# Weight splits in the attention stage, tied behind the last issued exponential

## The chip, the cores and the metric

The kernel runs on one NeuronCore of a Trainium2 chip. Its metric is the device time of one execution in microseconds (us), from launch to end. TensorE (PE) multiplies; PEld is the loading of its stationary operand, which overlaps it; VectorE (DVE), ScalarE (ACT) and GpSimd (POOL) work beside it; SyncE (SP) and POOL issue the DMAs. Each engine takes its instructions in one fixed order that is set when the program is built, and semaphores hold an instruction back until its operands are there.

## The reference, cut to what matters

The kernel computes two transformer-like blocks over 1024 tokens of width 1024, in float32. The stage that the change touches is the differential attention of the second block: eight heads, each with two score maps of head dimension 64, and values of width 128.

```python
q = rope_partial(rms_norm(q, q_norm), cos, sin) * (ATTN_HEAD_DIM ** -0.5)
k = rope_partial(rms_norm(k, k_norm), cos, sin)
for blk in range(s // Q_BLOCK):
    q0, q1 = blk * Q_BLOCK, (blk + 1) * Q_BLOCK
    sc = jnp.einsum('bqhmd,bkhmd->bhmqk', q[:, q0:q1], k[:, :q1])
    p = jax.nn.softmax(jnp.where(mask, sc, NEG_INF), axis=-1)
    w = p[:, :, 0] - lam * p[:, :, 1]
    outs.append(jnp.einsum('bhqk,bkhd->bqhd', w, v[:, :q1]))
o = rms_norm(jnp.concatenate(outs, axis=1), subln) * (1.0 - lambda_init)
mixed = sigmoid(g_lru) * y_lru + sigmoid(g_attn) * y_attn
```

q, k and v, and the two gates g_lru and g_attn, are products of the normalised input with slices of w_in.

## The kernel before, in words

A float32 product is made of three matmuls on split operands: a value is kept as a rounded high part and a low part, and high x high, high x low and low x high are added (`mm3`, lines 171 to 175). A weight is split where it is loaded: `stream` and `load_split` take one of two raw buffers, SP issues a DMA of 512 KB, ACT copies the rounded high part (tile wh) and DVE subtracts it from the raw data for the low part (tile wl). There are four buffers of wh and four of wl. The copy of wh therefore waits for the DMA and for the last matmul on the tile that had its buffer; the next DMA into the same raw buffer waits for DVE's subtraction.

Attention runs in four passes p of two heads each. A pass has 16 units: query tiles of 128 rows in the order 0, 7, 1, 6, 2, 5, 3, 4, taken in pairs, and for each pair both heads hh. A unit goes through these steps:

- `unit_qk` (line 1481): scores into PSUM (tile sc, two buffers), row maxima on DVE (tile st), and two exponentials on ACT (tile e, line 1528), one for each map.
- `unit_mix`: DVE combines the two maps in place in e.
- `unit_tr`: PE transposes the mixed weights (tile pt), ACT and DVE split them (wth, wtl).
- `unit_pv`: PE multiplies with V into tile po; `unit_o` adds the result on DVE.

Between the steps of units, `fill` takes work from a generator of fillers, which keeps PE busy while ACT and DVE work on a unit. The fillers are the key and value projections (`k_tiles`, tile pj, 24 matmuls of 128x256 for 128 rows), the query projections (`q_tile`, also pj) and the gate projections (`gate_unit`, tile pg, 24 matmuls of 128x512). The weights of k and v for a pass are asked for at the head of `k_tiles` through `w2` (four wh and wl tiles, two of k and two of v), those of q after the fourth value tile, and those of a gate through `gate_w`. `need` runs the rest of a pass's projections alone when the next pass begins.

The Python code states dependencies and priorities; a scheduler that works when the program is built puts the instructions of each engine in order. `issue_after(ins)` adds an edge: every instruction traced inside the block that runs on the engine of `ins` must stand behind `ins` in that engine's order. It adds no semaphore.

Of the kernel before, what the change touches and what calls it, by code (L numbers as in the profile page):

```python
# [16 lines left out]
AF = mybir.ActivationFunctionType  # L17
# [112 lines left out]
class Model:  # L130
# [906 lines left out]
    def lru(self):  # L1037
        nc, A = self.nc, self.A
        D = self.dram
        self.ghb = [D.tile([128, 1024], F32, name=f"gh{i}") for i in range(8)]  # L1040
        self.tab = [D.tile([128, 1024], F32, name=f"ta{i}") for i in range(16)]
        self.x0 = None
        self.w4p = self.pool("w4")
        W = self.w4 = self.w4p.__enter__()
        self.at0p = self.pool("at0")
# [153 lines left out]
    def attention(self):  # L1199
        nc, A = self.nc, self.A  # L1200
        self.ob = [self.dram.tile([128, 1024], F32, name=f"ob{i}") for i in range(8)]
        self.t0b = [self.dram.tile([128, 1024], F32, name=f"t0{i}") for i in range(8)]
        W = self.w4
        with self.pool("at1") as T1, self.pool("at") as T, \
# [8 lines left out]

            alone = [False, 0]

            def w2(src):
                return [self.stream(W, src[j], [128, 4, 256]) for j in range(2)]

            def proj(w, i, out):

# [49 lines left out]
            gst = {}  # L1270

            def gate_w(j):
                if j < 16 and j not in gst:
                    g, n = gates[j]
                    gst[j] = self.stream(W, A["w_gl2" if g == 0 else "w_ga2"][n], [128, 8, 128])

            def gate_unit(u):
                j, h = divmod(u, 2)
                g, n = gates[j]
                w = gst[j]  # L1280
                if u == 1:
                    ps = PS.tile([128, 512], F32, name="pg", tag="sc")
                else:
                    ps = PJ.tile([128, 512], F32, name="pg", tag="pj")
                for k in range(8):
                    self.mm3(ps, (w[0][:, k], w[1][:, k]), self.xnc(k, h), k == 0, k == 7)
                    if k == 3 and h == 0 and j % 4:
                        gate_w(j + 1)
                    yield 0.65
                t = T.tile([128, 512], F32, name="tg", tag="tg", bufs=1)  # L1290
                self.act(t, ps, AF.Tanh, scale=0.5)
                nc.gpsimd.dma_start(out=self.tab[8 * g + n][:, h * 512:h * 512 + 512], in_=t)
# [4 lines left out]

            def k_tiles(p):
                wk = w2(A["w_k2"][p])
                wv = w2(A["w_v2"][p])  # L1300
                yield "k", p
                kh = T.tile([128, 4, 1024], F32R, name="kh", tag="kh")
# [12 lines left out]
                for n in range(8 + 2):  # L1315
                    if n < 8:
                        o = []
                        yield from proj(wk, n, o)
                        d, _ = norm_rope(o[0], n, True)
                        pend.append((n, d))  # L1320
                    if n == 1:
                        yield "v", p
                    if n > 1:
                        j = n - 2
                        o = []
                        yield from proj(wv, j, o)
                        ps = o[0].rearrange("p (h a) b -> p h (a b)", h=2)
                        self.split(V[:, j, :, 0], V[:, j, :, 1], ps)
                        finish()
                        yield 0.3  # L1330
                        if j == 3:
                            WQ[p] = w2(A["w_q2"][p])
# [19 lines left out]
            def fillers():  # L1352

                gate_w(0)
                yield from gate_unit(0)
                yield from gate_unit(1)
                for p in range(4):
                    yield from k_tiles(p)
                    gate_w(4 * p + 1)
                    for n, i in enumerate(tiles):  # L1360
                        q = q_tile(p, i)
                        for c in q:
                            if c == -1:
                                break
                            yield c
                        if n > 1:
                            yield from gate_unit(8 * p + n)
                        else:
                            yield 0.1
                        yield from q  # L1370
                        yield "q", p, n

                    if p < 3:
                        yield from gate_unit(8 * p + 8)
                        yield from gate_unit(8 * p + 9)
# [105 lines left out]
    def unit_qk(self, unit, QS, KV):  # L1481
        nc = self.nc
        T, PS, PT, _, ma, mb, lamn, _ = self.at
        p, i, hh = unit
        self.mark(f"at{p}.{i}.{hh}")
        qs, rq = QS[p, i]
        kh, kl, _ = KV[p]
        W = (i + 1) * 128
        wc = max(W, 256)
        one = wc <= 512  # L1490
        pieces = [(0, wc)] if one else [(0, wc // 2), (512, wc // 2)]
        st = T.tile([128, 8], F32, name="st", tag="st", bufs=3)
        rqh = rq[:, 2 * hh:2 * hh + 2]
        es, vs = [], []
        sc = None
        for m in range(2):
            a = 2 * hh + m
            if m == 0 or not one:
                sc = PS.tile([128, 2, 512], F32, name="sc", tag="sc")
            base = sc[:, m] if one else sc.rearrange("p a b -> p (a b)")  # L1500
            k0 = 0
            for pi, (o, n) in enumerate(pieces):
                last = pi == len(pieces) - 1
                nc.tensor.matmul(base[:, o:o + n], qs[:, a], kh[:, a, k0:k0 + n], start=True, stop=False)
                nc.tensor.matmul(base[:, o:o + n], qs[:, a], kl[:, a, k0:k0 + n], start=False, stop=not last)
                if last:

                    end = 128 if i == 0 else o + n
                    nc.tensor.matmul(base[:, end - 64:end], ma, mb, start=False, stop=True)
                k0 += n  # L1510
            if not one:
                v = sc[:, :, 0:W // 2]
                nc.vector.tensor_reduce(out=st[:, m:m + 1], in_=v, op=OP.max, axis=AX.XY)
                self.stt(st[:, m:m + 1], st[:, m:m + 1], -1.0, rqh[:, m:m + 1], OP.mult, OP.mult)
            vs.append(sc[:, m, 0:W] if one else v)
        if one:
            nc.vector.tensor_reduce(out=st[:, 0:2], in_=sc[:, :, 0:W], op=OP.max, axis=AX.X)
            self.stt(st[:, 0:2], st[:, 0:2], -1.0, rqh, OP.mult, OP.mult)
        for m in range(2):
            e = T.tile([128, 512 if one else 1024], F32, name="e", tag=f"e{m}{int(one)}", bufs=1)  # L1520
            ev = e[:, 0:W] if one else e[:, 0:W].rearrange("p (a b) -> p a b", a=2)
            self.act(ev, vs[m], AF.Exp, bias=st[:, m:m + 1], scale=rqh[:, m:m + 1], accum=st[:, 2 + m:3 + m])
            es.append(e[:, 0:W])
        return {"st": st, "es": es, "i": i, "hh": hh, "po": None}

# [1028 lines left out]
```

## Time and profile before

| | |
|---|---|
| median of 3 runs | 2487.82 us (2479.79 to 2490.89) |
| profiled execution, its own time | 2485.62 us |
| span of that execution | 2483.9 us |
| PE busy | 2355.6 us, 95% |
| DVE busy | 1748.2 us, 70% |
| ACT busy | 1314.5 us, 53% |

The span is from the first to the last instruction. The attention stage takes the stretch from about 697 to 1440 us. The four passes have their first exponentials near 759, 939, 1118 and 1297 us. A busy PE is not PE at its peak, because matmuls overlap; its waits, with what ended them, are the more telling view. [...]

### The profile page before, as it was taken

How to read it: one execution, taken by the hardware profiler on the slowest of the kernel's cores; microseconds unless marked ns; L12 is line 12 of the kernel's file. 1: busy time of each engine (PE TensorE's matmuls, PEld its weight loads, DVE VectorE, ACT ScalarE, POOL GpSimd, SP SyncE). 2: the span in 40 equal slices, each digit the busy share in tenths (PEclk: the TensorE clock that was granted, in tenths of full speed). 3: DMA queues.
4: the chain of work that ended last, by engine and by line, in shares of the span. 5: the costliest groups of instructions: out<-in, count | busy, mean ns of one | idle time of the engine just before them, and what ended most of it. 6: DMA issues, size and time to landing. Idle time of an engine off the chain costs nothing. (4 is left out here: it accounts for less than half of the span.)

```text
span 2483.9 us, 35045 instructions
## 1 busy us (share of the span) xinstructions
PE 2355.6 (95%) x13016; PEld 1936.7 (78%) x13016; DVE 1748.2 (70%) x3344; ACT 1314.5 (53%) x2102; POOL 341.5 (14%) x363
## 2 busy tenths in 40 slices
PE   8999989999999999999899899999997999999998
PEld 6888868787888898798798678887885777666765
DVE  9667767677875666666666744235667999898987
ACT  5344532445645455454445432134435888787886
POOL 1011114100021021121121100000011111111111
PEclk9999999999999999999999999999998999999999
DMA  6322353322221111110111456532267999999992
GB/s 222 99 68 67 117 179 127 123 78 84 72 77 39 64 45 42 51 52 35 56 51 40 144 199 221 176 119 77 85 244 271 368 376 373 371 372 359 368 371 66
DMA packets 103838, 394.32 MB, mean 159 GB/s; under 512 B 14129, under 2 KB 33073, under 8 KB 79089
## 3 DMA queue, kind: packets, MB, share of 16 engines
q1 hardware_dynamic: 85008, 335.18, 37.5%
q0 software_dynamic: 18656, 56.88, 7.3%
q8 instruction: 104, 1.70, 0.3%
q14 instruction: 70, 0.57, 0.1%
HBM read 339.07 MB, written 61.31 MB: 161 GB/s over the span
## 5 line engine op out<-in xcount | busy, mean ns | idle before, releaser
L166 DVE TENSOR_TENSOR wl<-raw,wh 128x1024 fp32r<-128x1024 f32 (+1 forms) x496 | 587.7, 1209 | 130.3 <-ACT wh L154 126.1
L154 ACT ACTIVATE wh<-raw 128x1024 fp32r<-128x1024 f32 (+1 forms) x496 | 512.1, 1048 | 250.0 <-PE pj L174 67.2
L173 PE MATMUL pj<-wh,xnh 128*128 128x256 f32 x768 | 222.2, 289 | 2.1 <-ACT tg L154 1.0
L175 PE MATMUL pj<-wh,xnl 128*128 128x256 f32 x768 | 217.2, 283 | 0.0
L174 PE MATMUL pj<-wl,xnh 128*128 128x256 f32 x768 | 217.0, 283 | 0.0
L175 PE MATMUL pg<-wh,xl 128*96 128x512 f32 x512 | 201.3, 393 | 1.6 <-DVE xl L166 1.6
L174 PE MATMUL pg<-wl,xh 128*96 128x512 f32 x512 | 202.6, 396 | 0.0
L173 PE MATMUL pg<-wh,xh 128*96 128x512 f32 x512 | 200.2, 400 | 0.9 <-ACT xh L154 0.9
L173 PEld LDWEIGHTS pj<-wh,xnh 128*128 128x128 f32 x768 | 145.4, 189 | 3.8 <-ACT pc L154 2.5
L174 PEld LDWEIGHTS pj<-wl,xnh 128*128 128x128 f32 x768 | 145.2, 189 | 0.0
L175 PEld LDWEIGHTS pj<-wh,xnl 128*128 128x128 f32 x768 | 145.1, 189 | 0.0
L154 ACT ACTIVATE e<-sc,st,ss 128x1024 f32<-128x1024 f32 (+7 forms) x128 | 105.7, 829 | 54.2 <-DVE st L158 42.4
L178 POOL TENSOR_TENSOR ss<-ss,mhalf 128x4 f32<-128x4 f32 (+1 forms) x68 | 72.7, 1069 | 343.5 <-DVE ss L163 318.4
L173 PE MATMUL pd<-wh,ah 128*96 128x512 f32 x248 | 98.2, 400 | 16.6 <-ACT y L154 16.6
L175 PEld LDWEIGHTS pg<-wh,xl 128*96 128x96 f32 x512 | 83.1, 162 | 38.6 <-DVE xl L166 3.2
L173 PEld LDWEIGHTS pg<-wh,xh 128*96 128x96 f32 x512 | 83.0, 162 | 33.8 <-ACT xh L154 1.3
L174 PEld LDWEIGHTS pg<-wl,xh 128*96 128x96 f32 x512 | 82.8, 162 | 32.4
L173 PE MATMUL pg<-xnh,wh 128*128 128x512 f32 x256 | 104.9, 410 | 0.4 <-ACT kv L154 0.2
L175 PE MATMUL pg<-xnh,wl 128*128 128x512 f32 x256 | 102.6, 401 | 0.0
L173 PE MATMUL pj<-xnh,wh 128*128 128x512 f32 x256 | 102.2, 400 | 0.0
L174 PE MATMUL pg<-xnl,wh 128*128 128x512 f32 x256 | 102.2, 399 | 0.0
L174 PE MATMUL pj<-xnl,wh 128*128 128x512 f32 x256 | 101.2, 396 | 0.0
(998 smaller groups left out, 6327.5 us busy)
## 6 DMA issues: line engine op xcount, KB each, us to landing
raw<-in_w_gu SPq DMA_DIRECT2D x128, 1024.0 KB, 15.3
raw<-in_w_dn SPq DMA_DIRECT2D x64, 1024.0 KB, 15.9
raw<-in_w_out SPq DMA_DIRECT2D x16, 512.0 KB, 4.6
ta<-tg POOLq DMA_DIRECT2D x32, 256.0 KB, 2.5
t<-ta SPq DMA_DIRECT2D x14, 512.0 KB, 3.9
raw<-in_w_ga SPq DMA_DIRECT2D x12, 512.0 KB, 3.7
raw<-in_w_v SPq DMA_DIRECT2D x12, 512.0 KB, 3.5
xraw<-in_xT SPq DMA_DIRECT2D x8, 512.0 KB, 5.8
```

Of the source, the lines that this page charges most:

```text
L154: return self.nc.scalar.activation(out=out, in_=in_, func=func, **kw)
L166: return (eng or self.nc.vector).tensor_tensor(out=out, in0=a, in1=b, op=op)
L173: mm(ps, l[0], r[0], start=start, stop=False)
L174: mm(ps, l[0], r[1], start=False, stop=False)
L175: return mm(ps, l[1], r[0], start=False, stop=stop)
L178: self.nc.gpsimd.tensor_tensor(out=out, in0=in_, in1=self.mhalf[:, :w], op=OP.pow)
```

## The change

`unit_qk` now keeps the exponential that it issued last in `self.last_exp`. `w2` and `gate_w` open an `issue_after` block on it around their `stream` calls, if there is one. The last exponential runs on ACT, so the edge binds the ACT half of a split, the copy of wh; DVE's subtraction follows because it reads wh. The DMAs are on SP and are not bound.

```diff
-        self.x0 = None
+        self.x0 = self.last_exp = None
...
+            def after_exp():
+
+                return self.tc.issue_after(self.last_exp.ins) if self.last_exp else nullcontext()
+
             def w2(src):
-                return [self.stream(W, src[j], [128, 4, 256]) for j in range(2)]
+                with after_exp():
+                    return [self.stream(W, src[j], [128, 4, 256]) for j in range(2)]
...
-                    gst[j] = self.stream(W, A["w_gl2" if g == 0 else "w_ga2"][n], [128, 8, 128])
+                    with after_exp():
+                        gst[j] = self.stream(W, A["w_gl2" if g == 0 else "w_ga2"][n], [128, 8, 128])
...
-            self.act(ev, vs[m], AF.Exp, bias=st[:, m:m + 1], scale=rqh[:, m:m + 1], accum=st[:, 2 + m:3 + m])
+            self.last_exp = self.act(ev, vs[m], AF.Exp, bias=st[:, m:m + 1], scale=rqh[:, m:m + 1], accum=st[:, 2 + m:3 + m])
```

What this does to the orders is shown at two places, both at the end of the first pass. The first is ACT. In the kernel before, the copies wh_8653 and wh_8659 (key weights of the second pass) and wh_8665 (value weights) stand among the exponentials of the middle of the pass; e_8049 and e_8051 belong to query tile 2, e_8133 and e_8135 to tile 5.

```order
L154 ACTIVATE wh_8653<-raw_8655 128x1024
L154 ACTIVATE e_8049,st_8039<-sc_8040,st_8039,ss_7840 128x384
L154 ACTIVATE e_8051,st_8039<-sc_8040,st_8039,ss_7840 128x384
L154 ACTIVATE qs_8113<-pt_8108,gcol_5343 128x512
L154 ACTIVATE pc_8340<-pj_8315 128x256
L154 ACTIVATE wh_8659<-raw_8661 128x1024
L154 ACTIVATE nq_8343<-pc_8340 128x256
L154 ACTIVATE nr_8342<-pc_8340 128x512
L154 ACTIVATE wth_8141<-pt_8137 128x384
L154 ACTIVATE wh_8665<-raw_8667 128x1024
L154 ACTIVATE e_8133,st_8116<-sc_8117,st_8116,ss_8010 128x768
L154 ACTIVATE tg_8439<-pg_8354 128x512
```

In the changed kernel the same copies stand behind e_8624, the last exponential of the pass (query tile 4, second head), with the copy of the first key projection, pc_8783, behind all four.

```order
L154 ACTIVATE e_8622,st_8605<-sc_8606,st_8605,ss_8345 128x640
L154 ACTIVATE ot_8579<-pt_8574,sub_5339 128x512
L154 ACTIVATE e_8624,st_8605<-sc_8614,st_8605,ss_8345 128x640
L154 ACTIVATE wh_8653<-raw_8655 128x1024
L154 ACTIVATE wh_8659<-raw_8661 128x1024
L154 ACTIVATE wth_8631<-pt_8626 128x512
L154 ACTIVATE osq_8595<-o4_7549 128x512
L154 ACTIVATE wh_8665<-raw_8667 128x1024
L154 ACTIVATE wh_8671<-raw_8673 128x1024
L154 ACTIVATE pc_8783<-pj_8727 128x256
```

The copies moved past 16 exponentials (wh_8653) to 8 (wh_8671) on ACT; their subtractions on DVE moved with them. The second place is PE, a little ahead of that point, where it transposes the mixed weights of the unit of tile 3, first head (pt_8471 from e_8386). In the kernel before, the 24 matmuls of a key projection (pj_8836) stand in front of it, of which the first four are shown; po is a product with V, and pt_8442 turns a query tile.

```order
L1266 MATMUL pt_8442<-ident_60,nr_8342 128x128 x4
L1551 MATMUL po_8418<-V_6710,wtl_8403 128x256
L1550 MATMUL po_8418<-V_6710,wth_8402 128x256
L1551 MATMUL po_8418<-V_6710,wtl_8403 128x256
L173 MATMUL pj_8836<-wh_8653,xnh_3988 128x256
L174 MATMUL pj_8836<-wl_8654,xnh_3988 128x256
L175 MATMUL pj_8836<-wh_8653,xnl_3989 128x256
L173 MATMUL pj_8836<-wh_8653,xnh_3988 128x256
```

In the changed kernel the transposes and the next unit's scores follow the product with V directly (lines are six higher from `unit_qk` on).

```order
L1271 MATMUL pt_8442<-ident_60,nr_8342 128x128 x4
L1557 MATMUL po_8418<-V_6710,wtl_8403 128x256
L1556 MATMUL po_8418<-V_6710,wth_8402 128x256
L1557 MATMUL po_8418<-V_6710,wtl_8403 128x256
L1544 MATMUL pt_8471<-ident_60,e_8386 128x128 x4
L1510 MATMUL sc_8451<-kh_6708,qs_8447 128x320
L1511 MATMUL sc_8451<-kl_6709,qs_8447 128x320
```

Both key projections that stood between the units of the last two query tiles (pj_8727 and pj_8836, 48 matmuls) have left this stretch, and 16 matmuls of a third (pj_8797) have left the stretch after it; all now stand behind the transposes pt_8626 of the last unit but one. The ends of the second and third pass have the same moves (there 24 matmuls in place of the 16). The fourth pass has no next pass to project for.

## Rows read from the trace of the kernel before

**Rows 1.** The page's busy shares, and the clock granted in 40 slices.

```profile
PE 2355.6 (95%) x13016; PEld 1936.7 (78%) x13016; DVE 1748.2 (70%) x3344; ACT 1314.5 (53%) x2102; POOL 341.5 (14%) x363
...
PEclk9999999999999999999999999999998999999999
```

**Rows 2.** Waits of PE in the first three passes: total us, times, longest.

```profile
PE sc L1504 <- ACT e L154: 8.8, 6, 1.9
PE po L1551 <- DVE wtl L166: 6.3, 6, 1.6
PE pt L1538 <- DVE e L158: 1.8, 3, 1.4
PE po L1550 <- ACT wth L154: 1.7, 3, 0.6
```

**Rows 3.** Projections (tile pj) on PE before each pass's last units: length, busy, count.

```profile
857.80:865.50 7.70, 6.08 (x48) 1.00 0.32 104
1035.80:1043.50 7.70, 6.10 (x48) 1.00 0.32 105
1216.50:1224.10 7.60, 6.01 (x48) 1.00 0.30 103
```

**Rows 4.** The first pass's end, stretches: length; PE, PEld, DVE, ACT, POOL busy; PEclk.

```profile
857.80:865.50 7.70, 7.70 (x68) 7.70 (x67) 5.27 (x14) 3.28 (x8) 0.45 (x1) 1.00 0.32 104
865.50:873.90 8.40, 5.27 (x35) 3.92 (x33) 6.26 (x16) 2.96 (x6) 0.58 (x1) 1.00 0.00 0
873.90:881.70 7.80, 6.76 (x40) 6.12 (x41) 6.49 (x22) 4.44 (x10) 1.30 (x2) 0.78 0.00 0
881.70:891.00 9.30, 9.30 (x81) 9.30 (x80) 7.98 (x26) 5.24 (x13) 3.91 (x5) 1.00 0.15 59
```

**Rows 5.** Timeline of DVE there: start, us, operation.

```profile
862.29 0.75 DVE L158 SCALAR_TENSOR_TENSOR e<-e,st 128x512 f32<-128x512 f32 x1
863.49 0.76 DVE L158 SCALAR_TENSOR_TENSOR qs<-pt,gcol,qs 64x512 fp32r<-64x512 f32 x1
```

**Rows 6.** Timeline of PE there: transposes of the mixed weights, and one wait.

```profile
865.47 0.60 PE L1538 MATMUL pt<-ident,e 128*128 128x128 f32 x4
...
873.95 0.77 PE L1538 MATMUL pt<-ident,e 128*128 128x128 f32 x5 [1.41 <-DVE e L158]
...
881.73 0.60 PE L1538 MATMUL pt<-ident,e 128*128 128x128 f32 x4
```

**Rows 7.** Timeline of ACT: exponentials and square of the units of tiles 4 and 3.

```profile
869.45 0.89 ACT L154 ACTIVATE e<-sc,st,ss 128x640 f32<-128x640 f32 x1 [2.74 <-PE po L1551]
...
871.19 0.62 ACT L154 ACTIVATE osq<-o 128x512 f32<-128x512 f32 x1
...
881.15 0.89 ACT L154 ACTIVATE e<-sc,st,ss 128x640 f32<-128x640 f32 x1 [1.09 <-DVE oss L166]
```

**Rows 8.** Weight splits of the first three passes: count, busy us, mean ns, idle before.

```profile
L154 ACT ACTIVATE wh<-raw 128x1024 fp32r<-128x1024 f32 x26 | 27.6, 1060 | 28.5 <-PE pg L174 23.3 <-PE pj L175 5.2
L166 DVE TENSOR_TENSOR wl<-raw,wh 128x1024 fp32r<-128x1024 f32 x26 | 31.8, 1225 | 11.5 <-ACT wh L154 11.0
```

**Rows 9.** DMA issues of these passes: count, KB, median us to landing.

```profile
raw<-in_w_v SPq DMA_DIRECT2D x6, 512.0 KB, 3.5
```

**Rows 10.** Timeline of ACT at a split in mid-pass.

```profile
835.05 1.06 ACT L154 ACTIVATE wh<-raw 128x1024 fp32r<-128x1024 f32 x1 [5.91 <-PE pg L174]
836.01 0.97 ACT L154 ACTIVATE e<-sc,st,ss 128x768 f32<-128x768 f32 x1
836.98 0.58 ACT L154 ACTIVATE tg<-pg 128x512 f32<-128x512 f32 x1
837.46 0.99 ACT L154 ACTIVATE e<-sc,st,ss 128x768 f32<-128x768 f32 x1
```

**Rows 11.** Timeline of PE at the same place.

```profile
834.85 0.40 PE L175 MATMUL pg<-xnh,wl 128*128 128x512 f32 x1
837.13 0.44 PE L1504 MATMUL sc<-kh,qs 128*128 128x384 f32 x1 [1.88 <-ACT e L154]
```

## The prediction

> **What bounds the kernel now.** I read the page's busy shares first: PE is busy for 95% of the span and its clock is at the upper level in nearly every slice [rows 1]. So a time can only be gained by taking away PE's idle time or its half clock, and lost by adding to either. Next I read PE's waits in the three passes whose ends the change touches: 8.8, 6.3, 1.8 and 1.7 us, 18.6 us together [rows 2]. That is all the idle time that a better order could take away there. Then I asked what keeps PE busy at a pass's end, where both fillers and units run out. The projections do it: 48 matmuls, 6.08, 6.10 and 6.01 us, stand in the 7.7 us before the last units of each pass [rows 3], and there PE has no idle time at all (7.70 of 7.70). In the next 8.40 us, which hold no projections, PE is busy for only 5.27 [rows 4]. This second row shows what the units alone look like: PE waits for ACT and DVE.
>
> **What the change does.** Nothing is added to or removed from the arithmetic; 26 ACT copies of 1.06 us and 26 DVE subtractions of 1.23 us were there in these passes [rows 8] and are there after. They move. The block ties a split to the exponential that the code issued last. For the weights of keys and values that is the pass's very last exponential, because the code of the last unit's scores is run before the generator reaches the next `k_tiles`. So four copies per pass end, and the two key projections that need them, go from the middle of the pass to behind its end. I work out the first pass's end in four pieces; the orders of the other two ends move alike.
>
> Piece A, up to the transposes at 865.47 [rows 6]. Of the 7.7 us, 6.1 leave and 1.6 of PE work stay [rows 3, 4]. The transposes cannot follow at once: DVE finishes the mixture that they read at 862.29 + 0.75 = 863.04 [rows 5]. They can come 2.4 us earlier, so the piece is 5.3 long with 1.6 of work: 3.7 us idle, before none. The bounds are 0 (all 6.1 us come back because the softmax chain too moves forward) and 6.1 (nothing is shortened); the two rows give the value between.
>
> Piece B, to the next transposes at 873.95 [rows 6]. No filler stood here, and none does now. But the query's low part on DVE, 0.76 us, was done before the transposes of piece A, at 864.25 [rows 5], and now comes between the mixture and the next scores: 0.8. And in the new ACT order the square of 0.62 us, which stood behind two exponentials [rows 7], stands between them: 0.6. Together 1.4; bounds 0 (DVE, without the first key tile's normalisation, catches up) and 2.
>
> Piece C, to the transposes at 881.73 [rows 6]. Here 16 projection matmuls leave and the transposes move forward by as much as these took, since they only stood behind them in PE's order: 0. The upper bound is 1.9, 16 matmuls at 0.12 (6.08 over 48, about 0.125 each) with nothing gained.
>
> Piece D, behind the last exponential, which begins at 881.15 and takes 0.89 [rows 7]. In the kernel before PE had no idle time in the 9.30 us from there [rows 4]. Now the first projection waits for a copy of 1.06 and its low part for another 1.23 on DVE [rows 8]; DVE must first do the unit's own mixture, some 0.9 for 640 columns (estimate from 0.75 for 512 [rows 5]). And wth, which the product with V needs, stands behind two copies, 2 x 1.06 + 0.6 = 2.7 (the 0.6 an estimate from the square of the same width [rows 7]). So PE gets its stream back some 2.9 us after that exponential; it has transposes and a few matmuls till about then, but it reaches them half a microsecond before the exponential ends, now that nothing else delays it. I take 3.0; bounds 1.5 (only the copy's time and a wait) and 4.6 (two copies and two subtractions in a row).
>
> What hides the rest: the raw buffer of the value weights is freed by the first subtraction, at 2.9; then 3.5 us of DMA [rows 9], 1.06 and 1.23 make 8.7. Till then PE has the 48 postponed matmuls and eight products with V, 6.1 + 1.0 from 2.9 on, so till 10.0. It is covered with 1.3 us to spare, and counts nothing; beyond that, each us that the DMA is later costs one.
>
> The sum for one end: 3.7 + 1.4 + 0 + 3.0 = 8.1; for three ends 24.3.
>
> In mid-pass there is one place of 1.88 us idle [rows 11] per pass. ACT stood idle for 5.91 us behind a copy that waited for a buffer, and took 1.06 for it, while an exponential was ready that PE's scores waited for [rows 10]. The change puts that copy away: about 1.0 back. But the split of the pass's last gate weight now stands right behind the second exponential here, and PE, which runs out of gate matmuls, waits for 1.06 + 1.23 of it with only some scores and transposes to do: about 1.0 lost. I take 0, bounds -1.9 and +1.3.
>
> [...]
>
> [...] I assume as much half clock at each end as before, no more. [...]
>
> The last part of attention and the expert stage get slightly other orders too, since the scheduler starts from other times; I see no term in them that has a sign, and count 0, give or take 3.
>
> **The time.** The profiled execution took 2485.62 us, 1.7 over its span and 2.2 below the median of the runs shown, well inside their spread of 11. The sum is made against it: 2485.6 + 24.3 = 2509.9, so 2510.
>
> **The rivals.**
> - The early copies were the hindrance. For it: ACT's idle time of 28.5 us in front of copies [rows 8], and PE's 8.8 us behind exponentials [rows 2]. If those 8.8 go and the postponed projections are as good later, the time is 2476.8; if all 18.6 us of waits go, 2467.0. It decides from the point where the units' chain on ACT and DVE runs ahead of PE without help. Against it: [rows 4] shows that it does not run ahead, in just these stretches. This is the case on the other side; chance 0.10, of which 0.07 is beyond half a per cent.
> - The chain closes up. Without the key tile's normalisation DVE has less to do, so pieces A and B shrink: A 1.5, B 0, D 2.0, three times 3.5, gives 2496.1. For it: DVE is busy for 6.26 of 8.40 us and ACT for 2.96 [rows 4], so neither is full. Against: the steps follow each other, and a chain is not shortened by engines that are free between its steps. Chance 0.21.
> - The gap breeds more. Piece C pays its 1.9 and each end a further 1.7 of half clock: 8.1 + 3.6 = 11.7, three times, gives 2520.7. For it: the 0.78 behind a lesser gap [rows 4]. Against: the 1.88 us of mid-pass and its kind did not always bring a half clock; the means of the slices stay at 9 tenths or more [rows 1]. Chance 0.15.
> - That the change does not do what it says is excluded by the order: the four copies do stand behind the last exponential.
>
> **How the numbers follow.** The forecast has 0.54, with 2501 to 2517 as its own range (A from 2.5 to 4.5, B from 0.5 to 2, D from 2 to 4). A measurement here can tell about half a per cent, 12.4 us, from no change. Slower by more: the forecast and the third rival, 0.69. Within: the second rival and the small end of the first, 0.24. Faster by more: 0.07. The range for 8 in 10 goes from 2488, which takes in most of the second rival, to 2524, which takes in the third.
>
> **What would show it.** Right: at each of the three pass ends the four wh copies stand in ACT's timeline behind the pass's last exponential; between the units of the last two query tiles PE shows new waits, of 2 us and more before the transposes (for e on DVE) and before the scores (for e on ACT); then a wait of about 3 us at the first projection, for wh and wl; PE's waits in the three passes grow from 18.6 to about 40. The DMA of the value weights lands before PE asks for it. Wrong: if PE's waits there stay under 25, piece A has closed up; if the time is above 2524, look at the granted clock at the ends and at waits for the value weights; if it is below 2486, look whether the 1.88 us places have gone and the ends have not grown.

## The result and the profile after

The changed kernel takes 2517.3 us (median of 4 runs, 2515.24 to 2519.68) against 2488.2 us (4 runs, 2479.79 to 2490.89): ratio 1.0123, 95% interval [1.0097, 1.0149]. The forecast was 2510 in a range of 2488 to 2524. The profiled execution took 2517.62 us with a span of 2515.6, so there are 31.7 us of span to explain where the prediction had 24.3.

The page after, against [rows 1]: busy shares and granted clock.

```profile
PE 2367.7 (94%) x13016; PEld 1939.4 (77%) x13016; DVE 1748.3 (69%) x3344; ACT 1313.5 (52%) x2102; POOL 341.8 (14%) x363
...
PEclk9999999999999999999999999999998999999999
```

The instruction counts are those of before, and yet PE is busy for 12.1 us more: here busy time is no count of work, so a loss need not show as idle time alone.

Waits of PE in the three passes after (total, times, longest), against [rows 2]:

```profile
PE pt L1544 <- DVE e L158: 11.0, 6, 2.5
PE sc L1510 <- ACT e L154: 9.1, 12, 1.4
PE po L1556 <- ACT wth L154: 3.6, 6, 0.9
PE pt L1582 <- DVE wtl L166: 2.9, 2, 1.8
PE pj L173 <- ACT wh L154: 1.2, 1, 1.2
```

All groups of this view add to 31.4 us, before 18.6. The largest is the wait that the prediction named for piece A and B, transposes for the mixed weights of DVE. At the first pass's end PE's timeline has, against [rows 6]:

```profile
863.34 0.63 PE L1544 MATMUL pt<-ident,e 128*128 128x128 f32 x4 [1.33 <-DVE e L158]
868.03 0.50 PE L1510 MATMUL sc<-kh,qs 128*128 128x512 f32 x1 [1.35 <-ACT e L154]
872.91 1.33 PE L1544 MATMUL pt<-ident,e 128*128 128x128 f32 x5 [2.11 <-DVE e L158]
877.58 0.60 PE L1544 MATMUL pt<-ident,e 128*128 128x128 f32 x4
879.42 0.51 PE L173 MATMUL pj<-wh,xnh 128*128 128x256 f32 x2 [1.24 <-ACT wh L154]
880.85 0.38 PE L1556 MATMUL po<-V,wth 128*128 128x256 f32 x1 [0.93 <-ACT wth L154]
```

The first is the gap that the fillers had filled (piece A). The next two are in piece B, where no filler stood before either; there the kernel before had waits of its own, 1.41 us for the transposes [rows 6] and, before the scores:

```profile
870.48 0.50 PE L1504 MATMUL sc<-kh,qs 128*128 128x512 f32 x1 [1.07 <-ACT e L154]
```

They became 2.11 and 1.35. The last two lines of the changed kernel are the restart behind the last exponential. The other side of that restart is on ACT, against [rows 7]: exponential, two copies in a row (x2), and only then the copy of the attention weights that PE asks for.

```profile
877.45 0.88 ACT L154 ACTIVATE e<-sc,st,ss 128x640 f32<-128x640 f32 x1
...
878.32 1.99 ACT L154 ACTIVATE wh<-raw 128x1024 fp32r<-128x1024 f32 x2
880.22 0.58 ACT L154 ACTIVATE wth<-pt 128x512 fp32r<-128x512 f32 x1
...
884.74 1.06 ACT L154 ACTIVATE wh<-raw 128x1024 fp32r<-128x1024 f32 x1 [3.42 <-DMA raw<-in_w_v]
```

The copy of the value weights does wait for its DMA, 3.42 us, but no line of PE names it: from 880.85 to 892 PE's timeline marks no wait. That cover held.

The same 34 us of both kernels in three stretches (length; PE, PEld, DVE, ACT, POOL busy; granted clock; DMA), before and then after:

```profile
858.00:866.00 8.00, 8.00 (x70) 8.00 (x70) 5.07 (x14) 3.28 (x8) 0.95 (x1) 1.00 0.31 100
866.00:878.00 12.00, 7.83 (x45) 6.05 (x44) 9.63 (x29) 6.21 (x14) 1.09 (x2) 0.91 0.00 0
878.00:892.00 14.00, 14.00 (x115) 13.80 (x115) 11.10 (x35) 7.23 (x16) 5.14 (x6) 0.96 0.10 39
```

```profile
858.00:866.00 8.00, 6.11 (x42) 4.86 (x41) 5.99 (x13) 4.27 (x9) 0.54 (x1) 1.00 0.08 33
866.00:878.00 12.00, 8.51 (x45) 6.85 (x43) 8.93 (x27) 6.86 (x15) 1.92 (x2) 0.72 0.00 0
878.00:892.00 14.00, 11.84 (x96) 11.27 (x95) 11.10 (x24) 8.46 (x16) 2.48 (x4) 1.00 0.51 168
```

PE's idle time (length less busy) goes from 4.2 to 7.5 us, and the half clock ((1 - PEclk) x length) from 1.6 to 3.4: 5.1 us more together in these stretches; the whole end costs 5.7. Half clock stands for a granted clock of 0.50, as PEclk has it in the kernel before from 876 to 879 us: there the products with V of 128x256 start 0.21 us apart, where from 880 to 883, at 1.00, the projections of 128x256 start 0.12 apart.

Where all 31.7 us arise is read by setting the same exponential's start in both traces side by side. The shift of after against before grows by 0.8 up to the first end; by 5.7, 8.4 and 8.5 over the three ends (from the first exponential behind the mid-pass copy, 836.01 in [rows 10] and 836.75 in the changed kernel, and its counterparts, to the first one of the next pass: 938.96 became 945.38, 1118.18 became 1133.33, 1296.64 became 1320.64); by 0.3 and 0.4 between them; by 2.6 from there to the expert stage; by 5.5 in it (to the last y, 0.4 of it given back by the end of the span). The ends are 22.6 of it.

### The profile page after: what moved, and what is told of

It is laid out like the page before. It is cut to its first block, busy times and chain, and to the rows that moved or that the text cites. A ratio compares the mean times of both kernels' runs of the same rounds, so it can differ in the third digit from the quotient of the medians.

```text
span 2515.6 us, 35051 instructions
## 1 busy us (share of the span) xinstructions
PE 2367.7 (94%) x13016; PEld 1939.4 (77%) x13016; DVE 1748.3 (69%) x3344; ACT 1313.5 (52%) x2102; POOL 341.8 (14%) x363
## 5 line engine op out<-in xcount | busy, mean ns | idle before, releaser
L154 ACT ACTIVATE pc<-pj 128x256 f32<-128x256 f32 x96 | 36.5, 382 | 127.9 <-PE pj L175 123.5
```

The source lines that it names most:

```text
L154: return self.nc.scalar.activation(out=out, in_=in_, func=func, **kw)
```

## The experiments

In all of them a split keeps its arithmetic; only the exponential to which it is tied changes, so the order. "Ends" is the growth of the shift over the three ends, as above, in the profiled execution; "expert" the growth in the expert stage. "Idle" and "half clock" are PE's over the three ends in the same execution, from the exponential at 839.55 before (the next unit's first, behind the mid-pass place) and its counterparts to the first one of the next pass; the half clock is rough, about half a us an end, since PEclk has two digits. The kernel before, run beside them, had medians of 2487.82, 2487.51 and 2486.87. In the edits `exps[-1]` is the exponential issued last, so `exps[-9]` is the ninth from the end, with eight behind it; the expectations call it "nine before the last", and the names "nine back" and the like below stand for `exps[-9]` and its kind.

| keys and values tied to | gates, q | median us | ratio, 95% | ends | expert | idle | half clock |
|---|---|---|---|---|---|---|---|
| (the kernel before) | | | | 0 | 0 | 13.1 | 6.9 |
| last (the change) | last | 2517.3 | 1.0123 [1.0097, 1.0149] | 22.6 | 5.5 | 26.7 | 11.7 |
| free | last | 2502.4 | 1.0068 [1.0051, 1.0085] | 4.6 | 3.9 | 16.8 | 6.0 |
| last | free | 2515.5 | 1.0112 [1.0095, 1.0129] | 22.7 | 9.1 | 27.4 | 15.0 |
| last, one pass of three | free | 2492.6 | 1.0024 [1.0014, 1.0033] | 6.3 | -0.9 | 17.8 | 8.3 |
| values alone, last | free | 2493.9 | 1.0026 [1.0016, 1.0035] | 7.0 | 5.5 | 15.8 | 13.2 |
| third from the end (three back) | free | 2503.3 | 1.0068 [1.0054, 1.0082] | 10.9 | 9.7 | 20.6 | 9.3 |
| fifth (five back) | free | 2482.1 | 0.9978 [0.9968, 0.9989] | -0.6 | -0.6 | 16.8 | 0 |
| seventh (seven back) | free | 2483.9 | 0.9988 [0.9979, 0.9997] | -4.8 | 5.3 | 11.4 | 0 |
| ninth (nine back) | free | 2478.9 | 0.9965 [0.9951, 0.9979] | -2.6 | -1.1 | 12.0 | 5.9 |
| thirteenth (thirteen back) | free | 2490.0 | 1.0006 [0.9995, 1.0017] | 5.4 | 5.5 | 18.2 | 8.0 |
| values alone, thirteenth | free | 2485.8 | 0.9993 [0.9984, 1.0003] | -3.5 | 5.6 | 10.9 | 6.9 |
| ninth | last | 2494.8 | 1.0032 [1.0021, 1.0042] | -0.3 | 9.0 | 10.6 | 6.9 |

How far an "ends" figure can be read is shown by the kernel with one pass tied. Its first end is not touched: PE and ACT have the order of the kernel before there, and PE's waits agree within 0.02 us. Yet its shift fell by 2.5. First the kernel before, then that one:

```profile
839.55:938.96 99.41, 95.20 (x717) 89.57 (x716) 65.24 (x173) 49.70 (x104) 18.18 (x21) 0.97 0.14 49
840.67:937.55 96.88, 92.57 (x714) 87.15 (x713) 65.06 (x173) 49.50 (x104) 18.28 (x21) 1.00 0.14 49
```

The idle time is 4.2 and 4.3 us; the difference is the granted clock, 0.97 and 1.00. So one end of one execution can move by 2.5 us with no change of order, and the idle time is the steadier measure of an order.

**Which ties cost.** The first edit frees keys and values, the second frees gates and q instead:

```diff
-            def w2(src):
-                with after_exp():
+            def w2(src, tied=True):
+                with after_exp() if tied else nullcontext():
...
-                wk = w2(A["w_k2"][p])
-                wv = w2(A["w_v2"][p])
+                wk = w2(A["w_k2"][p], False)
+                wv = w2(A["w_v2"][p], False)
```

> Undoes one part: the splits of key and value weights are free again, those of query and gate weights stay tied. Theory (the loss is at the three pass ends, because the key projections that filled PE there were moved behind the last exponential): the three ends cost nothing, PE's waits before the transposes of the last units vanish, and only the other terms of the measured loss can stay, about 5 us in the expert stage and 3 in the fourth pass: 2488 to 2497 us. Rival (the gate splits, which now stand behind exponentials in mid-pass, hold the gate projections up): 2505 us or more.

> Does one part alone: the splits of key and value weights are tied, those of query and gate weights are not. Theory: nearly the whole loss, 23 us at the three ends and what the expert stage adds: 2509 to 2519 us, with the same waits at the ends as in the changed kernel. Rival (gate splits): 2486 to 2494 us.

With keys and values free 4.6 us of the ends' 22.6 stay; with only these tied all 22.7 are there, and PE's idle time is 16.8 and 27.4 us. So the ends' loss belongs to the keys and values. That the two sums agree so well is in part luck: the second kernel loses 8.9, 6.5 and 7.3 where the changed one loses 5.7, 8.4 and 8.5, with more half clock. Nor are its waits those of the changed kernel, as was expected: its order puts the next tile's scores ahead of the transposes at each end (at the first, scores at 861.18 and transposes at 863.75; in the changed kernel transposes at 863.34 and scores at 864.03), and its largest waits are those of the products with V for wth and wtl (5.6 and 4.6 us). But 2502.4 fits neither expectation: the gate ties have a price of their own, about 14 us by the medians. Of 11.8 us of span in the profiled execution 4.6 are at the ends and 3.9 in the expert stage.

**One end alone, and the values alone.** In both, gates and q are free as well. `p == 2` in place of `False` ties the keys and values of one pass. In the other kernel only `wv` is tied: the 48 key matmuls keep their place ahead of the last scores, and two copies stand behind the last exponential.

> Only the key and value splits of the third pass are tied, so one of three ends is changed. Theory: a third of the ends' loss, 8 us at the second end and none at the others, and up to 5 more if the expert stage takes the changed order: 2495 to 2503 us. Rival (the loss comes from a change of the scheduler's whole plan, not from each end): the first and third end move too, or the time is that of the changed kernel, 2510 us or more.

> Only the value weights' splits are tied, so the key projections keep their place between the last units while two of four copies and subtractions still come behind the last exponential, their DMAs being early. Theory (lost are the fillers, not the place of the copies): the ends cost 0 to 1 us each, 2488 to 2496 us with the expert stage's 5. Rival (late copies and subtractions themselves are the price, as in piece D of the prediction): 3 us or more at each end, 2500 us or more.

The tied end costs 8.1 us, the other two -2.5 and 0.8, and PE's idle time grows at the tied end alone (9.4 us, where the other two have 4.3 and 4.2): the ends are separate, and the prediction's multiplication by three holds. The time is below its range because of that -2.5, which is the clock's, and of 1.3 us gained in mid-pass. Values alone cost 1.7, 3.1 and 2.2 at the ends, between the 0 to 1 of the theory and the 3 of the rival, though the time is in the theory's range. Only 2.7 us of it is idle time of PE; the half clock grew by 6.3, where the untouched end above had 3.0 in one execution (0.97 over 99.41 us) and none in the other (1.00), so by an estimate up to 9 over three ends. So the price of late copies where the fillers stay is about 0.9 us of idle time an end, and up to 2.3 with a clock that this one execution doesn't settle.

**How late is too late.** Now keys and values are tied to an earlier exponential, with gates and q free:

```diff
-                return self.tc.issue_after(self.last_exp.ins) if self.last_exp else nullcontext()
+                return self.tc.issue_after(self.exps[-9].ins) if self.exps else nullcontext()
```

> Key and value weights stay tied, but to the exponential issued nine before the last instead of to the last; gate and query weights are free. So the four copies stand some 15 us before the pass's last units, no longer spread over mid-pass, and the 48 key projections are again between the last units but two. Theory (an end costs about 8 us because these matmuls have left the last units' gaps and because their copies come too late behind the last exponential): ends cost 0 to 2 us each, the mid-pass place of 1.88 us gains about 1.3 per pass as in the runs with only key and value weights tied, the expert stage -1 to +5: 2483 to 2493. Rival (it is the tie itself, four copies in a row ahead of a unit's work on ACT and DVE, wherever it stands): 5 us or more per end, 2500 to 2512.

> The same, tied to the exponential issued five before the last. The key projections now stand one unit later than before, between the last two units (pieces C and D filled, A and B empty). Theory (pieces A and B cost what they cost in the changed kernel, 3 to 4 us per end together, piece D with its late copies costs nothing, less 1.3 in mid-pass; expert stage -1 to +5): 2490 to 2503, between the nine-back and the last-exponential versions. Rival (the loss is all at the restart behind the last exponential, pieces A and B close up): 2483 to 2490, as with nine back. Rival (any delay costs the whole): above 2508.

> Key and value weights tied to the exponential thirteen before the last, gate and query weights free: the key projections now stand one unit earlier than before, and the stretch in front of the last units (piece A) has none of the second block. Theory (fillers are worth most where the units alone leave PE idle, which is in the last four units; earlier there are gate matmuls to fill): ends cost 0 to 3 us each, mid-pass -1.3: 2484 to 2495. Rival (earlier is never worse): at or below the nine-back version and at most 2486.

Nine back came out 4 us below its range and faster than both kernels: its ends gained 2.6 us where they were to cost 0 to 2 each. Five back missed: the key matmuls have left pieces A and B there too, as in the changed kernel, and yet the shift over its ends doesn't grow. Its 34 us at the first end:

```profile
858.00:866.00 8.00, 4.54 (x30) 3.62 (x30) 6.13 (x15) 3.83 (x10) 0.00 (x0) 1.00 0.00 0
866.00:878.00 12.00, 10.95 (x82) 10.03 (x83) 10.48 (x22) 8.66 (x16) 0.30 (x1) 1.00 0.39 125
878.00:892.00 14.00, 13.53 (x112) 13.14 (x112) 10.64 (x37) 6.56 (x16) 6.32 (x7) 1.00 0.19 64
```

Piece A is as idle as predicted, 3.5 us, but all 48 matmuls now run from 866 to 878, where the kernel before itself waited for 4.2 us. And the clock is at its upper level throughout. Total lost there: 5.0 us, against 5.8 before and 10.9 after. But the clock hides a part: by idle time its three ends cost 3.7 us (16.8 against 13.1). Pieces A and B are thus a small price by themselves; a filler is worth nearly as much in the last gap as in those ahead, so long as it comes ahead of the last scores. The kernel to compare with is not the changed one but keys and values alone, tied to the last: five back too has the next tile's scores ahead of the transposes (861.23 and 863.81). In these two, and in three back, the units' own matmuls have one order on PE up to the last scores, and only the fillers' place differs. Thirteen back, in its range, has half of the key projections one unit earlier and is worse again, by 8.0 us over the ends and 6.2 of idle time against nine back. But there the transposes come ahead of the scores, as in the kernel before, and in nine back behind them; so it is not shown that the fillers' place is the cause.

> Key and value weights tied to the exponential three before the last, gate and query weights free. The copies come just ahead of the last two exponentials, so that the projections can start right behind the last scores (piece D of the prediction is filled), but the 48 key projections and 16 of the others are still gone from the stretch before (pieces A to C stay empty). Theory (both halves count: the units' chain, which does not shorten by the 8 us of PE work that left it, costs 3.6 to 5.2 per end by the shift of the last exponential in the changed kernel, the restart behind it 2 to 4): 3.5 to 5.5 per end, -1.3 per pass in mid-pass, expert stage -3 to +5: 2490 to 2502. Rival (all of the loss is the restart): as with five back, 2479 to 2486. Rival (all of it is the chain): 2505 or more.

> The same, seven before the last: the 48 key projections stand between the units of the last two query tiles, one place later than with nine back. Theory (where in the last units the fillers stand does not matter, so long as all of them stand ahead of the last scores): 2477 to 2484, as five and nine back. Rival (each position has its own cost): 2487 or more.

Three back is the counterpart of the values alone. The two copies of the key weights stand ahead of the last two exponentials, so that the projections are ready in time, but the 48 fillers still come behind the last scores (and the copies of the value weights behind the last exponential). The restart is mended (PE busy for all 14.00 us from 878), the gaps ahead are not:

```profile
858.00:866.00 8.00, 4.71 (x22) 3.00 (x20) 5.18 (x15) 4.30 (x10) 0.00 (x0) 0.77 0.00 0
866.00:878.00 12.00, 9.02 (x41) 7.51 (x41) 9.05 (x23) 6.30 (x12) 1.03 (x1) 0.73 0.01 1
878.00:892.00 14.00, 14.00 (x122) 14.00 (x121) 13.00 (x36) 8.25 (x17) 5.59 (x6) 1.00 0.55 188
```

Side by side at the second end: the kernel before, then keys and values tied to the last exponential, three back and five back.

```profile
1019.08:1118.18 99.10, 94.91 (x714) 89.59 (x713) 64.53 (x173) 49.30 (x103) 18.57 (x20) 0.97 0.14 48
1027.86:1133.46 105.60, 96.27 (x714) 89.97 (x713) 69.34 (x176) 52.79 (x107) 17.76 (x21) 0.97 0.17 56
1021.47:1123.47 102.00, 94.99 (x714) 88.60 (x713) 68.24 (x176) 52.66 (x106) 18.33 (x21) 0.98 0.17 58
1017.87:1116.82 98.95, 93.11 (x714) 87.44 (x713) 68.27 (x176) 52.02 (x106) 19.30 (x21) 1.00 0.18 60
```

PE has 714 recorded matmuls in each, and idle time of 4.2, 9.3, 7.0 and 5.8 us. Over three ends three back costs 7.5 us of idle time, keys and values tied to the last 14.3, the values alone 2.7: about half of the loss is the empty gaps, about a fifth the late copies of the values, and the rest comes only with both. (The shares are rough: three back's value copies are late too.) Its time was 1 us above the expected range, with 9.7 us in the expert stage. Seven back came in at the top of its range, with the best ends of all, -4.8, and 5.3 lost in the expert stage. But the place is not all one: its idle time is 5.4 us below that of five back.

**The place in mid-pass.** With values tied thirteen back and the rest free, PE's order at the ends is that of before up to the transposes behind the last scores, and on ACT the copy of [rows 10] has moved behind its exponentials.

> Only the value weights are tied, to the exponential issued thirteen before the last; keys, gates and queries are free. On PE the order at the pass's end is that of the kernel before; on ACT the one copy that stood idle for 5.91 us ahead of a ready exponential now stands behind it. Theory (head of the queue in ACT's order costs PE about 1 to 1.3 us at that place, once a pass, and nothing else changes): 2482 to 2486. Rival (the place's wait is paid again right behind it, since the same gate matmuls follow): 2487 to 2489. The expert stage's order may add -1 to +5 to either.

PE's wait there, against [rows 11], and then the three that the changed kernel has in its place:

```profile
836.18 0.44 PE L1510 MATMUL sc<-kh,qs 128*128 128x384 f32 x1 [0.84 <-ACT e L154]
```

```profile
837.88 0.44 PE L1510 MATMUL sc<-kh,qs 128*128 128x384 f32 x1 [0.60 <-ACT e L154]
839.35 0.44 PE L1510 MATMUL sc<-kh,qs 128*128 128x384 f32 x1 [0.33 <-ACT e L154]
841.77 0.44 PE L1510 MATMUL sc<-kh,qs 128*128 128x384 f32 x1 [0.75 <-ACT e L154]
```

1.88 us became 0.84, and the shift gains 1.0 to 1.1 us at this place in each pass; the time, 2485.8, is in the range, though its interval just reaches no change, since the expert stage takes 5.6 back. In the changed kernel the three waits add to 1.68: the gain was spent on the gate split, which now stands there. Keys and values alone, whose gate splits are free, do gain 1.3 there.

But no exponential was ready during the 5.91 us in front of the copy [rows 10], as the prediction and this expectation have it. First DVE in the kernel before, finishing the value from the row maxima that the exponential reads, then ACT in the kernel with the copy moved:

```profile
834.70 0.15 DVE L158 SCALAR_TENSOR_TENSOR st<-st,ss 128x1 f32<-128x1 f32 x1
```

```profile
835.05 0.99 ACT L154 ACTIVATE e<-sc,st,ss 128x768 f32<-128x768 f32 x1 [5.81 <-DVE st L158]
```

The exponential's operands were there at 834.85, 0.2 us before the copy began, and without the copy ACT stands idle just as long, now for DVE. What the copy cost there is its own 1.06 us, not the wait in front of it; so ACT's idle time in front of copies, which the first rival counts for itself, does not tell what they hold up.

**The change mended in one point.** Keys and values nine back, gates and q tied to the last exponential as in the change:

> The changed kernel with one thing undone: key and value weights are tied nine exponentials back, gate and query weights to the last one, as in the changed kernel. Theory (the gate ties cost what they cost alone, about 14 us with free keys and values, of which 1.3 to 2.9 per pass in mid-pass, some 2 in the last part of attention and 4 in the expert stage; no more of the loss remains): 2487 to 2495. Rival (the gate ties cost mostly through the keys and values that they push): 2478 to 2484.

The ends are free (-0.3, with 2.5 us less idle time). 2494.8 is at the top of the expected range: of the 12.8 us that the span grew in the profiled execution, 9.0 are in the expert stage, and 4.1 are left for all outside it and the ends.

## Why the prediction was right

The range and the sign held; the time was 7 us above the forecast and just above the forecast's own range of 2501 to 2517. By its own pieces, from the shifts of the transposes of [rows 6] and of their counterparts at the other two ends, which are in PE's timeline before

```profile
1043.45 0.60 PE L1538 MATMUL pt<-ident,e 128*128 128x128 f32 x4
...
1050.71 0.77 PE L1538 MATMUL pt<-ident,e 128*128 128x128 f32 x5 [0.17 <-DVE e L158]
...
1061.94 0.60 PE L1538 MATMUL pt<-ident,e 128*128 128x128 f32 x4
...
1224.14 0.60 PE L1538 MATMUL pt<-ident,e 128*128 128x128 f32 x4
...
1231.93 0.77 PE L1538 MATMUL pt<-ident,e 128*128 128x128 f32 x5 [0.17 <-DVE e L158]
...
1240.39 0.60 PE L1538 MATMUL pt<-ident,e 128*128 128x128 f32 x4
```

and after

```profile
1048.86 0.63 PE L1544 MATMUL pt<-ident,e 128*128 128x128 f32 x4 [1.33 <-DVE e L158]
...
1058.31 0.77 PE L1544 MATMUL pt<-ident,e 128*128 128x128 f32 x5 [2.46 <-DVE e L158]
...
1064.69 1.05 PE L1544 MATMUL pt<-ident,e 128*128 128x128 f32 x4
...
1236.85 0.63 PE L1544 MATMUL pt<-ident,e 128*128 128x128 f32 x4 [1.33 <-DVE e L158]
...
1246.29 0.77 PE L1544 MATMUL pt<-ident,e 128*128 128x128 f32 x5 [2.46 <-DVE e L158]
...
1251.92 0.60 PE L1544 MATMUL pt<-ident,e 128*128 128x128 f32 x4
```

Each piece's loss is the growth of the shift over it, plus the time of the projections that left it (48 of [rows 3] in A; 16, 24 and 24 in C, 2.16, 3.86 and 2.94 us), less that of those that came back (D). The shift at the start of the three ends is 0.75, 6.72 and 15.51. For A at the first end: 863.34 - 865.47 - 0.75 + 6.08 = 3.2.

| piece | forecast | first end | second | third |
|---|---|---|---|---|
| A | 3.7 | 3.2 | 4.8 | 3.2 |
| B | 1.4 | 1.1 | 2.2 | 1.7 |
| C | 0 | -1.0 | -1.0 | 0.1 |
| D | 3.0 | 2.6 | 3.3 | 3.5 |

- **A, B and D** were right, in place and size: three ends make 22.6 by the shifts where the forecast had 24.3. D's parts stand in the trace as named: two copies in a row, then wth. But the forecast counted all of it as idle time, and of the 22.6 only some 13.6 are (26.7 against 13.1); the rest is busy time of PE, about 4.8 of it half clock. That the sum came out so near is in part luck. The signs that were named came out smaller too: at the first end 1.35 us before the scores, and 1.24 at the first projection where about 3 was expected. **C** was a microsecond better at two ends; at the first, the products' waits for wth and wtl, 0.58 and 0.41 us in the kernel before, are gone. (The pieces add to 23.7, the shifts to 22.6: some of the matmuls that came back had run at half clock before, as in [rows 4].)
- **What the pieces mean** was wrong. They were priced as if each gap had its own cost; five back shows that A may stay empty at little loss (3.7 us of idle time over three ends, against 14.3) if the fillers come in C. The terms that the runs bear out are two: no filler ahead of the last scores (2.5 us of idle time an end, by three back), and copies behind the last exponential (0.9, by the values alone); of the 4.8 an end with both, 1.4 belongs to neither by itself.
- **The value weights' DMA** cost nothing, as forecast. Its median was 4.1 us, not 3.5.
- **Mid-pass, 0**: right, 0.3 to 0.4 a pass, and by the terms given: the copy's removal is worth 1.0 to 1.1 a pass (values alone, thirteen back), and the gate split takes it again. But the reading behind it was wrong: the 5.91 us were no time that an exponential lost. What the trace shows is an exponential with its operands there at 834.85 that began at 836.01, behind the copy, which began at 835.05 and took 1.06 [rows 10].
- **PE's waits of about 40** were too many: 31.4. The pieces include half clock and other growth of PE's busy time that no wait shows. But they are above the 25 that would have spoken for the second rival.
- **The clock**: as many half-clock stretches as before is not decided. The half clock of the three ends went from 6.9 to 11.7 us, 1.6 more an end, where the forecast had 0 and the third rival 1.7, which is (1 - 0.78) x 7.80 of [rows 4]; but one untouched end moved by 2.5 us by the clock alone. The rival's other half, 1.9 more in C, went the other way.
- **The mis-sized term** is the one counted 0 give or take 3: the last part of attention and the expert stage cost some 8 us (2.6 and 5.5). In the expert stage the down projections (tile pd) wait more often for y, ACT's copy of an earlier one out of PSUM. That line of PE's waits from 1840 us on, for the kernels before, after, nine back and keys and values alone:

```profile
PE pd L173 <- ACT y L154: 16.6, 12, 1.7
```

```profile
PE pd L173 <- ACT y L154: 19.3, 14, 1.7
```

```profile
PE pd L173 <- ACT y L154: 14.8, 11, 1.7
```

```profile
PE pd L173 <- ACT y L154: 19.7, 15, 1.7
```

Over all thirteen profiles the expert stage's growth goes by this count: 11 or 12 waits with -1.1 to 0, 14 with 3.9 to 5.6, 15 with 9.0 to 9.7. No edit touched that stage; the scheduler orders it anew in each build. That the waits cause the growth was not tested, nor why an order falls one way or the other; it stays open. Of the 6.6 us of span that nine back gains, 1.1 lie there, 2.6 at the ends and 2.9 in the rest of attention.

The first rival, that the early copies were the hindrance, was right in kind and wrong in size: at the 1.88 us place a copy was in the way, by its own time, and a tie that is neither so early nor so late, nine back, beats both kernels. But only 1 us a pass lay there, not 8.8.

## What to carry to other kernels

Here work that fills the gaps of a waiting chain had to be ready ahead of the chain's last step; in which of the gaps it started mattered less (3.7 us of idle time over three ends five back, 14.3 tied to the last). Tied behind that last step, it cost the gaps and a restart besides (2.5 and 0.9 us of idle time an end, and 1.4 that belongs to neither by itself). So when an order edge is added, look at which matmuls need the moved instruction, not at the instruction. And where a scheduler orders the whole program, read a difference stage by stage: a stage that no edit touched moved here by -1 to +10 us. And a stage's time in one execution holds the clock of that execution, 2.5 us of it at the untouched end; idle time at equal work, 4.2 and 4.3 us there, is the steadier reading.

## What was not expected of the hardware

With five back the granted clock over the three passes was 1.00 in two digits, against 0.98 before, though PE's idle time in the first end was more than before (5.0 against 4.2 us, from the stretches above); the passes, first before and then five back:

```profile
757.00:1240.00 483.00, 463.66 (x3120) 414.05 (x3119) 309.90 (x797) 239.08 (x500) 71.12 (x82) 0.98 0.14 47
```

```profile
757.00:1240.00 483.00, 463.75 (x3156) 413.73 (x3157) 312.22 (x810) 241.70 (x508) 74.16 (x83) 1.00 0.14 47
```

PE's busy time is the same, with 36 matmuls more in it. Seven back has no half clock at its ends either (0 in the table, with 11.4 us of idle time), and the untouched first end of the kernel with one pass tied had none, with the order and the idle time of the kernel before (1.00 against 0.97; 4.3 and 4.2 us). So neither the idle time nor the order alone decides it. Each profile is one execution: over the executions run side by side the mean granted clock was 0.982 to 0.988 with five back (12 executions) and 0.979 to 0.986 before (28, without one of 4937.86 us), so the two overlap. What brings the half clock, these runs don't show.
